# Layer norms: mean and variance from VectorE's statistics instruction on each half, second steps half by half

## The chip, the cores and the metric

One core of one Trainium2 chip runs the whole program; the other seven are idle. The metric is device time in microseconds (us), the median of repeated executions. The engines named below are PE (TensorE, matrix products), DVE (VectorE, elementwise work and reductions along a row), ACT (ScalarE, one-input functions), POOL (GpSimd) and SP (SyncE, which only issues transfers here).

## The reference, cut to what matters

The model is a first block (mixers and a gated feed-forward network with RMS norms) followed by a second block of two layers. All activations are 256 x 1024 in float32. The second block normalizes after each of its three sublayers, so there are six layer norms in all:

```python
def _layer_norm(x, g, b):
    xf = x.astype(F32)
    mu = jnp.mean(xf, axis=-1, keepdims=True)
    xc = xf - mu
    var = jnp.mean(xc * xc, axis=-1, keepdims=True)
    return (xc * lax.rsqrt(var + LN_EPS) * g.astype(F32) + b.astype(F32)).astype(x.dtype)

for i in range(DEPTH_2):          # 2 layers: NSA attention, then HGRN2
    x = _layer_norm(alpha * x + 0.5 * _swiglu(x, ffn1...), ln_gain[i, 0], ln_bias[i, 0])
    y = _nsa(...) if kind == 0 else _hgrn2(...)
    x = _layer_norm(alpha * x + y, ln_gain[i, 1], ln_bias[i, 1])
    x = _layer_norm(alpha * x + 0.5 * _swiglu(x, ffn2...), ln_gain[i, 2], ln_bias[i, 2])
```

## The kernel before, in words

**Tiling.** The 256 positions are two tiles (tt = 0 and 1) of 128 partitions; a row's 1024 features lie along the free axis, in two halves of 512 (hf = 0 and 1), because a product of one tile accumulates in two PSUM banks, `acc[0]` and `acc[1]`.

**Products.** Every weight is split into a high and a low part: ACT copies it to `hi` (line 262), DVE subtracts to get `lo` (line 265), and `bulk_mm` (line 355) multiplies both. `get()` hands out the next weight and splits up to five halves ahead; there are six buffers for `hi` and three for each `lo`, so a split can also wait until PE has used an older weight. The activations are split in the same way: `to_XT` transposes four 128 x 128 blocks on PE (line 513), which is one half of a tile, and `split_to` makes the high part on ACT (line 500) and the low part on DVE (line 503) into `XT`.

**The layer norm.** `ln_tile` is called once for each tile of each of the six norms, so 12 times. It forms `r` = alpha x + product, half by half (line 566, with a running sum into `st`); three steps on one column per row follow (lines 568, 570, 571), which scale the sum to the mean and set the extra column of `r` from which the epsilon comes. ACT then squares the whole centred row of 1025 columns into a scrap tile `jk` and adds it up (line 574); POOL raises the result to the power -1/2 (line 536 in `rsqrt`); DVE subtracts the mean and multiplies by the gain, both halves (line 578, "sub" below), and multiplies by the root and adds the bias, both halves (line 581, "mul" below). `to_XT` transposes the result for the next product; the last norm writes each half to DRAM instead.

**Where the norms stand.** After a feed-forward network (sites A, C, D and, at the end, F) a stock of held products lets PE finish tile 0 long before tile 1. After the two mixers (site B after NSA attention, site E after HGRN2) `Out.last` finishes tile 0 first, and only the remaining products of tile 1 are left for PE (`n1` of 8 steps are already done): `W.last(fin)` calls `finish(tt, ...)`, that is `ln_tile`, after each tile. The next product, `mmB_first`, takes tile 0 for all four weight halves and then tile 1.

**What sets the order.** The instructions are not issued in the order of the text. A planner goes through simulated time and gives each engine, whenever it is free, the ready instruction with the best priority; `tc.high_priority(offset=PRI)` puts the norms ahead of the weight splits around them. The order so planned is then fixed: each engine works through its own queue in that order. `queue_behind(i, other)` adds an edge for order only. `behind(ns, ...)` queues the transposes of `to_XT` behind so many nanoseconds of bulk products; `LNNS` = 4600 for tile 0 and 4300 for tile 1 after a feed-forward network, 0 and 4300 after a mixer, plus 600 for the second half.

Of the kernel before, what the change touches and what calls it, by code (L numbers as in the profile page):

```python
# [9 lines left out]
F32 = mybir.dt.float32  # L10
F32R = mybir.dt.float32r
U32 = mybir.dt.uint32
AF = mybir.ActivationFunctionType
ALU = mybir.AluOpType
# [3 lines left out]
P = 128  # L18
S = 256
D = 1024  # L20
DFF = 2816
NEG = -1e30
ALPHA = 4.0 ** 0.25
# [83 lines left out]
def _kern(ctx, tc, nc, A, out):  # L107
    V, ACT, PE, POOL = nc.vector, nc.scalar, nc.tensor, nc.gpsimd
    cp = ctx.enter_context(tc.tile_pool(name="cp", bufs=1))
    wp = ctx.enter_context(tc.tile_pool(name="wp", bufs=4))  # L110
    xp = ctx.enter_context(tc.tile_pool(name="xp", bufs=2))
# [3 lines left out]
    def nm(s):  # L115
        _n[0] += 1
        return f"{s}_{_n[0]}"


    def new_x(rms=False):  # L120

        t = xp.tile([P, D + 1], F32, tag="x", bufs=3, name=nm("x"))
        if rms:
            POOL.memset(t[:, D : D + 1], 32.0 * 1e-6 ** 0.5)
        return t
# [19 lines left out]
    def queue_behind(i, other):  # L145

        tc.add_manual_dep(i, other.ins.name,
                          mybir.DependencyInfo(mybir.DependencyClass.NoSync, mybir.DependencyReason.DATA))
# [360 lines left out]
    def to_XT(XT, tt, x, k0=0, nk=8, ns=0, gain=None):  # L509
        for q in range(0, nk, 4):  # L510
            w = min(4, nk - q)
            ps = psb()
            ts = [PE.transpose(ps[:, j * P : (j + 1) * P], x[:, (q + j) * P : (q + j + 1) * P], ident) for j in range(w)]  # L513
            if ns:
                behind(ns + 150 * q, [t.ins for t in ts])
            ks = slice(k0 + q, k0 + q + w)
            src = ps[:, : w * P].rearrange("p (a b) -> p a b", a=w)
            if gain is None:
                split_to(XT[:, ks, tt, 0, :], XT[:, ks, tt, 1, :], src)
            else:  # L520
                ACT.activation(XT[:, ks, tt, 0, :], src, AF.Copy, scale=gain)
                V.scalar_tensor_tensor(XT[:, ks, tt, 1, :], src, gain, XT[:, ks, tt, 0, :].bitcast(F32), ALU.mult, ALU.subtract)
# [6 lines left out]
    def rsqrt(src, n, eps):  # L529

        r = xp.tile([P, 16], F32, tag="rsr", bufs=4, name=nm("rsr"))
        if eps:
            v = xp.tile([P, 16], F32, tag="rsv", bufs=4, name=nm("rsv"))
            POOL.tensor_scalar(v[:, :n], src, float(eps), None, ALU.add)
            src = v[:, :n]
        POOL.tensor_tensor(r[:, :n], src, mhalf[:, :n], ALU.pow)  # L536
        return r[:, :n]
# [15 lines left out]
    def load_gb(g, b):  # L553
        t = xp.tile([P, 2, D], F32, tag="gb", bufs=1, name=nm("gb"))
        nc.sync.dma_start(t[:, 0, :], g.partition_broadcast(P))
        if b is not None:
            nc.sync.dma_start(t[:, 1, :], b.partition_broadcast(P))
        return t

    def ln_tile(tt, x, acc, gb, XT, final=False, ns=0):  # L560
        y = new_x()
        r = xp.tile([P, D + 1], F32, tag="r", bufs=2, name=nm("r"))
        st = xp.tile([P, 4], F32, tag="st", bufs=4, name=nm("st"))
        for hf in range(2):
            cs = slice(hf * 512, (hf + 1) * 512)
            V.scalar_tensor_tensor(r[:, cs], x[:, cs], ALPHA, acc[hf], ALU.mult, ALU.add, accum_out=st[:, hf : hf + 1])

        V.tensor_scalar(st[:, 2:3], st[:, 0:1], st[:, 1:2], 1.0 / (32 * D), ALU.add, ALU.mult)

        V.tensor_scalar(r[:, D : D + 1], st[:, 2:3], 32.0, 32.0 * 1e-5 ** 0.5, ALU.mult, ALU.add)  # L570
        V.tensor_scalar(st[:, 3:4], st[:, 2:3], 32.0, None, ALU.mult)
        jk = xp.tile([P, D + 1], mybir.dt.bfloat16, tag="jk", bufs=1, name=nm("jk"))
        var = xp.tile([P, 1], F32, tag="ss", bufs=4, name=nm("var"))
        ACT.activation(jk, r, AF.Square, bias=st[:, 2:3], scale=-1.0 / 32, accum_out=var)  # L574
        rs = rsqrt(var, 1, 0)
        for hf in range(2):
            cs = slice(hf * 512, (hf + 1) * 512)
            V.scalar_tensor_tensor(y[:, cs], r[:, cs], st[:, 3:4], gb[:, 0, cs], ALU.subtract, ALU.mult)
        for hf in range(2):
            cs = slice(hf * 512, (hf + 1) * 512)  # L580
            V.scalar_tensor_tensor(y[:, cs], y[:, cs], rs, gb[:, 1, cs], ALU.mult, ALU.add)
            if final:
                nc.sync.dma_start(out[tt * P : (tt + 1) * P, cs], y[:, cs])
        if not final:
            to_XT(XT, tt, y, ns=ns)
        return y
# [917 lines left out]
    x = list(x0)  # L1504
# [23 lines left out]
    for li in range(2):  # L1528
        gb = load_gb(A["ln_gain_2"][li, 0:1], A["ln_bias_2"][li, 0:1])
        XT, XTn = XTn[0], [newXT()]  # L1530

        def fin(tt, acc, ns):
            with tc.high_priority(offset=PRI):
                x[tt] = ln_tile(tt, x[tt], acc, gb, XTn[0], ns=ns)

        ffn(XT, False, True, fin)
        gb = load_gb(A["ln_gain_2"][li, 1:2], A["ln_bias_2"][li, 1:2])
        XT, MT = XTn[0], newXT()
        W = Out(MT, N1[1 + li])
        (nsa_mix if li == 0 else hgrn_mix)(XT, MT, W)  # L1540
        XTn = [newXT()]
        W.last(fin)
        gb = load_gb(A["ln_gain_2"][li, 2:3], A["ln_bias_2"][li, 2:3])
        XT, XTn = XTn[0], [newXT() if li == 0 else None]
        if li == 1:
            def fin(tt, acc, ns):
                with tc.high_priority(offset=PRI):
                    ln_tile(tt, x[tt], acc, gb, None, final=True)
        ffn(XT, False, True, fin)
# [42 lines left out]
```

## Time and profile before

| | |
|---|---|
| median of 3 executions | 1399.06 us (1398.65 to 1399.69) |
| profiled execution: its own time | 1401.19 us |
| its span, first to last instruction | 1399.0 us |
| PE busy | 1369.6 us (98%) |
| DVE busy | 947.4 us (68%) |
| ACT busy | 721.7 us (52%) |
| POOL busy | 35.6 us (3%) |
| mean granted clock of PE | 0.993 |

The span is what the trace covers; 2.19 us of the profiled execution lie around it. Busy shares are means over stages: an engine with a modest share can be the one that everything waits for in a short stretch.

### The profile page before, as it was taken

How to read it: one execution, taken by the hardware profiler on the slowest of the kernel's cores; microseconds unless marked ns; L12 is line 12 of the kernel's file. 1: busy time of each engine (PE TensorE's matmuls, PEld its weight loads, DVE VectorE, ACT ScalarE, POOL GpSimd, SP SyncE). 2: the span in 40 equal slices, each digit the busy share in tenths (PEclk: the TensorE clock that was granted, in tenths of full speed). 3: DMA queues.
4: the chain of work that ended last, by engine and by line, in shares of the span. 5: the costliest groups of instructions: out<-in, count | busy, mean ns of one | idle time of the engine just before them, and what ended most of it. 6: DMA issues, size and time to landing. Idle time of an engine off the chain costs nothing.

```text
span 1399.0 us, 21630 instructions
## 1 busy us (share of the span) xinstructions
PE 1369.6 (98%) x8649; PEld 1220.1 (87%) x8649; DVE 947.4 (68%) x1611; ACT 721.7 (52%) x1161; POOL 35.6 (3%) x65
## 2 busy tenths in 40 slices
PE   6999999999999999999999999999999999999997
PEld 6988999998888889998888888888889998888886
DVE  4865698877565776786765676555676666755574
ACT  4744544453545643776555463555645443555561
POOL 1010000000000000000000000000000000100000
PEclk9999999999999999999999999999999999999999
DMA  7623866555565665531665573565655332655560
GB/s 223 228 91 111 251 214 208 181 181 170 193 196 193 212 204 148 202 95 56 217 190 197 185 250 136 193 197 187 210 188 181 121 121 92 202 190 181 187 204 30
DMA packets 185427, 245.36 MB, mean 175 GB/s; under 512 B 7408, under 2 KB 164761, under 8 KB 185327
## 3 DMA queue, kind: packets, MB, share of 16 engines
q1 hardware_dynamic: 184511, 240.74, 52.9%
q0 software_dynamic: 816, 3.25, 0.8%
q8 instruction: 68, 1.11, 0.3%
q14 instruction: 32, 0.26, 0.1%
HBM read 242.89 MB, written 4.23 MB: 177 GB/s over the span
## 4 chain that ended last, share of the span: by engine, by line
PE 88%; issue 7%; DVE 2%; POOL 1%; ACT 1%; DMA 1%; SPq 0%; DVEq 0%; POOLq 0%; ACTq 0%
PE psa L355 37%; PE acc L355 23%; PE psb L355 20%; PE psb L513 1%; POOL rsr L536 1%; PE psb L1240 1%; DMA x<-in_x_dram 1%; PE psT L1223 1%; PE psS L1073 1%; PE psb L1242 1%; PE psS L1194 1%; DVE lo L265 0%; ACT hi L262 0%; PE psT L1225 0%; PE lev L1384 0%
## 5 line engine op out<-in xcount | busy, mean ns | idle before, releaser
L265 DVE TENSOR_TENSOR lo<-raw,hi 128x1024 fp32r<-128x1024 f32 x428 | 521.1, 1223 | 268.9 <-ACT hi L262 266.4
L262 ACT ACTIVATE hi<-raw 128x1024 fp32r<-128x1024 f32 x428 | 448.9, 1056 | 379.7 <-PE psa L355 143.1
L355 PE MATMUL psa<-XT,hi 128*128 128x256 f32 (+1 forms) x1632 | 413.5, 328 | 0.0
L355 PE MATMUL psa<-XT,lo 128*128 128x256 f32 x1136 | 321.6, 283 | 0.0
L355 PEld LDWEIGHTS psa<-XT,hi 128*128 128x128 f32 x1632 | 275.0, 188 | 30.2 <-issue 0.6
L355 PE MATMUL psb<-XT,hi 128*128 128x512 f32 (+1 forms) x960 | 283.8, 356 | 0.0
L355 PE MATMUL acc<-hi,H 128*128 128x512 f32 x880 | 280.3, 391 | 0.0
L355 PE MATMUL psb<-XT,lo 128*128 128x256 f32 x800 | 223.6, 279 | 0.0
L355 PEld LDWEIGHTS psa<-XT,lo 128*128 128x128 f32 x1136 | 214.3, 189 | 3.2 <-issue 1.2
L355 PE MATMUL psa<-hi,XT 128*128 128x256 f32 (+1 forms) x928 | 199.4, 304 | 0.6 <-ACT XT L500 0.6
L355 PEld LDWEIGHTS acc<-hi,H 128*128 128x128 f32 x880 | 165.3, 188 | 34.6
L355 PEld LDWEIGHTS psb<-XT,hi 128*128 128x128 f32 x960 | 169.1, 187 | 28.7
L355 PE MATMUL acc<-lo,H 128*128 128x512 f32 x440 | 172.8, 393 | 0.0
L355 PEld LDWEIGHTS psa<-hi,XT 128*128 128x128 f32 x928 | 151.6, 193 | 6.3 <-ACT XT L500 2.0
L355 PEld LDWEIGHTS psb<-XT,lo 128*128 128x128 f32 x800 | 150.2, 188 | 0.0
L355 PE MATMUL psa<-lo,XT 128*128 128x256 f32 (+1 forms) x464 | 130.9, 299 | 0.2 <-DVE lo L265 0.2
L355 PEld LDWEIGHTS acc<-lo,H 128*128 128x128 f32 x440 | 82.8, 188 | 16.7
L355 PEld LDWEIGHTS psa<-lo,XT 128*128 128x128 f32 x464 | 89.8, 194 | 2.4 <-DVE lo L265 0.5
L500 ACT ACTIVATE XT<-psb 128x512 fp32r<-128x512 f32 (+1 forms) x46 | 23.5, 531 | 46.6 <-PE psb L513 46.5
L500 ACT ACTIVATE H<-sg 128x512 fp32r<-128x512 f32 x51 | 31.6, 619 | 29.3 <-DVE sg L625 15.4
L659 ACT ACTIVATE sg<-z 128x512 f32<-128x512 f32 x40 | 25.2, 631 | 40.3 <-DVE z L442 40.1
L574 ACT ACTIVATE jk<-r,st 128x1025 bf16<-128x1025 f32 x12 | 13.9, 1156 | 48.3 <-DVE r L570 24.6
(353 smaller groups left out, 1208.2 us busy)
## 6 DMA issues: line engine op xcount, KB each, us to landing
raw<-in_ffn_w_gate_dram SPq DMA_DIRECT2D x44, 1024.0 KB, 5.1
raw<-in_ffn_w_up_dram SPq DMA_DIRECT2D x44, 1024.0 KB, 5.2
raw<-in_ffn_w_down_dram SPq DMA_DIRECT2D x44, 1024.0 KB, 4.8
raw<-in_w_up_dram SPq DMA_DIRECT2D x22, 1024.0 KB, 4.9
raw<-in_hgrn_w_in_dram SPq DMA_DIRECT2D x16, 1024.0 KB, 5.2
raw<-in_w_down_dram SPq DMA_DIRECT2D x11, 1024.0 KB, 5.2
raw<-in_nsa_w_in_dram SPq DMA_DIRECT2D x10, 1024.0 KB, 5.3
raw<-in_w_in_dram SPq DMA_DIRECT2D x9, 1024.0 KB, 5.0
```

Source lines behind the costliest of these rows:

```text
L262: h = ACT.activation(hi, src, AF.Copy)
L265: i = (POOL if j in pool_halves else V).tensor_tensor(lo, src, hi.bitcast(F32), ALU.subtract)
L355: i = PE.matmul(o, l, r, start=start, stop=stop)
L500: i = ACT.activation(hi, src, AF.Copy)
L513: ts = [PE.transpose(ps[:, j * P : (j + 1) * P], x[:, (q + j) * P : (q + j + 1) * P], ident) for j in range(w)]
L536: POOL.tensor_tensor(r[:, :n], src, mhalf[:, :n], ALU.pow)
L659: ACT.activation(sg, zg, AF.Silu)
L1073: PE.matmul(ph[:, 0:60], w1[:, l % 8, :], d["blk"][kv][:, l].rearrange("p c r n -> p (c r n)"), start=(l == 0), stop=(l == 15))
L1194: PE.matmul(s1, QS[:, j // 2, j % 2, P:S], K[:, u].rearrange("p a b -> p (a b)"), start=(i == 0), stop=(i == 1))
L1223: PE.transpose(pt[:, o : o + P], E1[:, br, sb * P : (sb + 1) * P], ident)
L1240: PE.matmul(po5[:, 1, j % 2, br], T1[:, 2 * br + sb], vv[br][:, sb, vs], start=(sb == 0), stop=(sb == 1))
L1242: PE.matmul(po5[:, 0, j % 2, br], T0[:, br], vv[br][:, 0, vs], start=True, stop=True)
```

## The change

The sum at line 566 is no longer taken. After each half of `r` is formed, DVE's statistics instruction (`bn_stats`) writes six numbers for that half into `st`, and `bn_aggr` joins the two sets to a mean and a variance. A small DVE step adds the epsilon, and POOL takes the power as before. ACT's square is gone, with its scrap tile. The last four DVE steps are put half by half: sub and mul of the first half, then sub and mul of the second, with an edge that keeps sub of the second half behind mul of the first.

```diff
-        st = xp.tile([P, 4], F32, tag="st", bufs=4, name=nm("st"))
+        st = xp.tile([P, 16], F32, tag="st", bufs=4, name=nm("st"))
         for hf in range(2):
             cs = slice(hf * 512, (hf + 1) * 512)
-            V.scalar_tensor_tensor(r[:, cs], x[:, cs], ALPHA, acc[hf], ALU.mult, ALU.add, accum_out=st[:, hf : hf + 1])
-        V.tensor_scalar(st[:, 2:3], st[:, 0:1], st[:, 1:2], 1.0 / (32 * D), ALU.add, ALU.mult)
-        V.tensor_scalar(r[:, D : D + 1], st[:, 2:3], 32.0, 32.0 * 1e-5 ** 0.5, ALU.mult, ALU.add)
-        V.tensor_scalar(st[:, 3:4], st[:, 2:3], 32.0, None, ALU.mult)
-        jk = xp.tile([P, D + 1], mybir.dt.bfloat16, tag="jk", bufs=1, name=nm("jk"))
-        var = xp.tile([P, 1], F32, tag="ss", bufs=4, name=nm("var"))
-        ACT.activation(jk, r, AF.Square, bias=st[:, 2:3], scale=-1.0 / 32, accum_out=var)
-        rs = rsqrt(var, 1, 0)
+            V.scalar_tensor_tensor(r[:, cs], x[:, cs], ALPHA, acc[hf], ALU.mult, ALU.add)
+            V.bn_stats(st[:, 6 * hf : 6 * hf + 6], r[:, cs])
+        V.bn_aggr(st[:, 12:14], st[:, 0:12])
+        V.tensor_scalar(st[:, 14:15], st[:, 13:14], 1e-5, None, ALU.add)
+        rs = rsqrt(st[:, 14:15], 1, 0)
+        done = None
         for hf in range(2):
             cs = slice(hf * 512, (hf + 1) * 512)
-            V.scalar_tensor_tensor(y[:, cs], r[:, cs], st[:, 3:4], gb[:, 0, cs], ALU.subtract, ALU.mult)
-        for hf in range(2):
-            cs = slice(hf * 512, (hf + 1) * 512)
-            V.scalar_tensor_tensor(y[:, cs], y[:, cs], rs, gb[:, 1, cs], ALU.mult, ALU.add)
+            i = V.scalar_tensor_tensor(y[:, cs], r[:, cs], st[:, 12:13], gb[:, 0, cs], ALU.subtract, ALU.mult)
+            if done is not None:
+                queue_behind(i.ins, done)
+            done = V.scalar_tensor_tensor(y[:, cs], y[:, cs], rs, gb[:, 1, cs], ALU.mult, ALU.add)
```

## Rows read from the trace of the kernel before

**Rows 1.** The page, busy time of each engine over the span.

```profile
PE 1369.6 (98%) x8649; PEld 1220.1 (87%) x8649; DVE 947.4 (68%) x1611; ACT 721.7 (52%) x1161; POOL 35.6 (3%) x65
```

**Rows 2.** Stages: us, busy PE, PEld, DVE, ACT, POOL, PE clock, DMA share, GB/s.

```profile
655.00:680.00 25.00, 23.72 (x142) 20.10 (x141) 22.88 (x39) 14.58 (x19) 1.40 (x2) 1.00 0.42 147
841.00:867.00 26.00, 26.00 (x156) 22.98 (x155) 15.52 (x32) 7.60 (x13) 1.10 (x2) 1.00 0.34 121
1190.00:1214.00 24.00, 21.46 (x129) 18.20 (x129) 19.17 (x37) 13.06 (x25) 3.84 (x6) 0.93 0.51 164
```

**Rows 3.** Timeline of PE, tile 0's transposes at sites B and E.

```profile
670.42 1.29 PE L513 MATMUL psb<-ident,x 128*128 128x128 f32 x8 [1.22 <-DVE x L581]
...
1202.80 1.75 PE L513 MATMUL psb<-ident,x 128*128 128x128 f32 x8 [2.00 <-DVE x L581]
```

**Rows 4.** Timeline of all engines at the end of the program, site F.

```profile
1391.03 0.69 DVE L566 SCALAR_TENSOR_TENSOR r<-x,acc 128x512 f32<-128x512 f32 x1 [3.06 <-PE acc L355]
...
1391.76 0.21 DVE L568 TENSOR_SCALAR st<-st 128x1 f32<-128x1 f32 x1
...
1392.26 1.15 ACT L574 ACTIVATE jk<-r,st 128x1025 bf16<-128x1025 f32 x1 [6.97 <-DVE st L571]
1392.26 1.41 DVE L578 SCALAR_TENSOR_TENSOR x<-r,st,gb 128x512 f32<-128x512 f32 x2
...
1393.64 0.54 POOL L536 TENSOR_TENSOR rsr<-var,mhalf 128x1 f32<-128x1 f32 x1 [7.73 <-ACT jk L574]
1394.22 1.41 DVE L581 SCALAR_TENSOR_TENSOR x<-x,rsr,gb 128x512 f32<-128x512 f32 x2 [0.55 <-POOL rsr L536]
```

**Rows 5.** Timeline of DVE at site C, tile 0.

```profile
848.73 0.69 DVE L566 SCALAR_TENSOR_TENSOR r<-x,acc 128x512 f32<-128x512 f32 x1 [2.89 <-PE acc L355]
...
852.49 1.41 DVE L581 SCALAR_TENSOR_TENSOR x<-x,rsr,gb 128x512 f32<-128x512 f32 x2 [0.43 <-POOL rsr L536]
```

**Rows 6.** Chain that ended last, site C: transposes of tile 0's second half.

```profile
855.50 0.44 PE psb L513 x4
```

**Rows 7.** Timeline of DVE at site E, tile 0 and the start of tile 1.

```profile
1197.49 0.68 DVE L566 SCALAR_TENSOR_TENSOR r<-x,psa 128x512 f32<-128x512 f32 x1
...
1198.26 0.69 DVE L566 SCALAR_TENSOR_TENSOR r<-x,psa 128x512 f32<-128x512 f32 x1
...
1199.44 0.69 DVE L566 SCALAR_TENSOR_TENSOR r<-x,acc 128x512 f32<-128x512 f32 x1
...
1200.05 1.41 DVE L578 SCALAR_TENSOR_TENSOR x<-r,st,gb 128x512 f32<-128x512 f32 x2
1201.90 1.42 DVE L581 SCALAR_TENSOR_TENSOR x<-x,rsr,gb 128x512 f32<-128x512 f32 x2 [0.44 <-POOL rsr L536]
```

**Rows 8.** Groups of DVE instructions by form: count, busy us, mean ns, idle before.

```profile
L751 DVE TENSOR_REDUCE ass<-kn 128x8 f32<-128x520 f32 x2 | 1.4, 686 | 0.0
...
L712 DVE TENSOR_SCALAR mT<-mT 128x512 f32<-128x512 f32 x1 | 0.4, 421 | 0.0
...
L1064 DVE TENSOR_TENSOR blk<-psa,posT 64x480 f32<-64x480 f32 x8 | 8.5, 1061 | 4.5 <-PE psa L355 4.4
```

**Rows 9.** Timeline of POOL at site E, tile 0's power.

```profile
1200.76 1.11 POOL L536 TENSOR_TENSOR rsr<-var,mhalf 128x1 f32<-128x1 f32 x1 [6.88 <-ACT jk L574]
```

**Rows 10.** Timeline of DVE at site B, tile 0 and part of tile 1.

```profile
665.84 0.68 DVE L566 SCALAR_TENSOR_TENSOR r<-x,psa 128x512 f32<-128x512 f32 x1
...
669.52 1.41 DVE L581 SCALAR_TENSOR_TENSOR x<-x,rsr,gb 128x512 f32<-128x512 f32 x2 [0.44 <-POOL rsr L536]
...
672.67 0.20 DVE L568 TENSOR_SCALAR st<-st 128x1 f32<-128x1 f32 x1
...
673.51 1.21 DVE L265 TENSOR_TENSOR lo<-raw,hi 128x1024 fp32r<-128x1024 f32 x1
```

**Rows 11.** Stages around the transposes of B and E, columns as in rows 2.

```profile
672.00:674.00 2.00, 2.00 (x18) 1.95 (x18) 2.00 (x8) 0.72 (x2) 0.00 (x0) 1.00 0.00 0
...
1204.00:1205.00 1.00, 1.00 (x6) 0.78 (x5) 0.65 (x2) 0.73 (x2) 0.00 (x0) 0.50 0.00 0
```

## The prediction

> **What bounds the kernel now.** I read the page first: PE is busy 98% of the span [rows 1], so the norms can cost time only where PE stands still for them. The stage table shows where. At site C, as at A and D, PE is busy in all of 26 us, while at B it misses 1.28 us of 25 and at E 2.54 us of 24 [rows 2]. The timeline of PE names the gap: tile 0's transposes come after 1.22 us of waiting at B and 2.00 us at E, both times for mul of line 581 [rows 3]. The fourth place is the end, F: after the last product DVE's work from 1391.03 to 1395.63 is bare, and the store of the last half follows it [rows 4]. So three short stretches decide: B, E and F. At B, moreover, DVE is nearly full, 22.88 of 25 us, while ACT is busy for 14.58 [rows 2]: there the change takes work from the engine with room and gives it to the one without.
>
> At A, C and D the norm has slack. At C, tile 0's second half is ready at 852.49 + 1.41 = 853.90 [rows 5], and its transposes, queued behind bulk products, begin at 855.50 [rows 6].
>
> **Prices.** Two rules come from the timelines. A DVE step that waits for nothing starts 0.08 us before the one in front ends (1199.44 + 0.69 against 1200.05 [rows 7]); so one sub or mul lasts (1.41 + 0.08) / 2 = 0.75 us. A step that waits for the one in front starts 0.04 after its end (1391.72 to 1391.76 [rows 4]).
>
> bn_stats is nowhere in the trace. It reads 512 numbers in each row and writes six. Below lies a one-input step on 128 x 512 at 0.42 us, above the slowest step of that length, 1.06 us for 480 numbers; the reduction of 520 numbers to 8 took 0.69 us [rows 8]. It is the nearest in what it reads and writes, so I take 0.69, with 0.42 and 1.06 for the range. bn_aggr and the step with the epsilon work on a few columns: 0.21 us each, as line 568 [rows 4]; at half or twice that each moves a site by 0.1 to 0.2, inside the bounds of bn_stats.
>
> **What goes.** The three small steps: from 1391.76 to 1392.26, 0.50 us. ACT's square and its readout, with the handoff: from 1392.26 to POOL's start at 1393.64, 1.38 us. But under these ran both subs, 1.41 us [rows 4]. The work that ACT loses is itself worth nothing: at B and E it has idle time, elsewhere PE covers it. The readouts of the running sum (0.08 each) were mostly inside the steps' own time; I count nothing for them.
>
> **What comes.** Per tile DVE gets two bn_stats (0.61 apiece when they don't wait), bn_aggr and epsilon (0.25 + 0.17) and loses 0.50: 1.14 us more. And the edge puts sub of the second half behind mul of the first, which waits for POOL. Before, both subs filled that wait. What is queued behind it now is the whole second half, and the transposes behind that.
>
> The wait is also longer than POOL's 0.54 us [rows 4]. At E the power began at 1200.76, under the second sub (which ended at 1200.05 + 1.41 = 1201.46 [rows 7]), and took 1.11 us [rows 9], to 1201.87: 0.41 after that sub ended. At F nothing ran beside it and it took 0.54. In the new order the power always meets sub of the first half, since DVE goes straight on to it after the epsilon. I therefore let the power end 0.41 after that sub.
>
> The Trainium skill, "SBUF — State Buffer", section "Summary: rules for kernel authors", speaks against the change here: when a VectorE instruction with two SBUF inputs runs beside a GpSimd instruction that reads SBUF, the later to issue is blocked until the first has finished. By that rule the power would run its whole 0.54 us after the sub, 0.13 more per norm than by the row, and the sum below would be about 0.4 us larger, an estimate by that page; the row decides.
>
> **F, worked out.** First step 1391.03 to 1391.72, bn_stats to 1392.45, bn_aggr to 1392.70, epsilon to 1392.95; sub of the first half from 1392.87 to 1393.62, power to 1394.03, mul from 1394.07 to 1394.82; then sub from 1394.74 and mul from 1395.53 to 1396.28. Before: 1395.63. **+0.6 us** (0.65; +0.24 without the meeting on POOL).
>
> **B.** Tile 0 from 665.84 [rows 10] by the same rules, in the order r, r, statistics, statistics: the second bn_stats ends at 668.35, bn_aggr 668.60, epsilon 668.85, sub 669.52, power 669.93, mul 670.72, then sub and mul to 672.18. Before, the mul steps ended at 670.27 and 670.93. The first half comes 0.45 late, the second 1.25; PE's order has all eight transposes ahead of the next product, so 1.25 is lost. Tile 1 has 1.14 more too, partly under tile 0's products: I count 0.5. That is 1.75 if DVE does nothing else meanwhile. But the planner fills the pauses of a chain that waits on itself: on tile 1 at B a weight split of 1.21 us stands between its small steps and its subs (673.51) [rows 10], and at E tile 1's first step stands at 1199.44, ahead of tile 0's subs [rows 7]. The new chain has more pauses: after the second bn_stats, after bn_aggr, before each mul. With a 0.61 us step of tile 1 in each (0.61 + 0.61 + 0.16 + 0.57) tile 0 comes 3.2 late, and tile 1 then costs nothing more. Between 1.75 and 3.2 I take **+2.3 us**: some are filled.
>
> **E.** Here the second half of r starts only at 1198.26, held by PE, so the first bn_stats is nearly free: it pushes that step to 1198.82. Then bn_stats to 1200.24, sub of the first half to 1201.41, power to 1201.82, mul to 1202.61 (before 1202.65), and the second mul to 1204.07 (before 1203.32). The second four transposes began at about 1202.80 + 1.75 / 2 = 1203.68 [rows 3] and would begin 0.15 behind that mul, at 1204.22: +0.54. Unlike before, this has no step of tile 1 in between; with one, as there was, +1.15, with all four +2.5. I take **+1.1 us**.
>
> **A, C, D.** At C the new chain from 848.73 [rows 5] ends at 855.08 instead of 853.90; 0.27 of the slack is left, after 0.15 for the handoff. A step of tile 1 ahead of the last mul would cost 0.57 and so 0.3 of a stall. For the three sites 0 to 0.9; I take **+0.3 us**, one of three. If statistics cost more than 0.82 us this cover is gone everywhere.
>
> **Sum.** 2.3 + 1.1 + 0.3 + 0.6 = 4.3 us. The profiled execution would go from its own 1401.19 us to 1405.5 (span 1399.0 to 1403.3); it lies 2.1 us above the median of the runs, so for the median 1399.06 + 4.3 = **1403.4 us**, 0.3% slower.
>
> **Rivals.**
> *The pauses stay empty.* 1.75 + 0.54 + 0 + 0.65 = 2.9 us at 0.69 per statistics; at 0.42 it falls by 1.0 at B, 0.5 at E and 0.3 at F, to 1.1. So 1400.2 to 1402.0. For it: before, tile 0 at B had none of tile 1's steps in its pauses [rows 10]. Against: its chain was shorter than tile 1's remaining products, the new one is longer. Chance 0.25.
>
> *Cheap statistics, a free POOL, and so a faster kernel.* If bn_stats runs at 0.42 and POOL isn't held by the sub, E's first mul ends at 1201.66, 1.0 earlier. PE's wait shrinks from 2.00 to about 1.0. After 2.00 us its clock fell to 0.50, the level of 1.2 GHz, and 6 products passed in 1 us; after 1.22 us at B the clock stayed at 1.00, 18 in 2 us [rows 3, 11]. Without the fall E gains 0.46 on the transposes and about 0.7 behind them, with an earlier second half some 1.5; B loses 0.3, F nothing: 1397.9 us. It decides below 0.45 us per statistics and only if POOL is free. Against it: the 1.11 us of rows 9. Chance 0.12, of it 0.05 under 1396.3.
>
> *All pauses filled, or dear statistics.* 3.2 + 2.5 + 0.9 + 0.65 = 7.25: 1406.3 us; with B's wait grown to that of E and the same fall of the clock about 1.1 more. At 1.06 us per statistics the sum of 4.3 rises by 1.5 + 0.7 + 0.4 + 1.4 to 8.3: 1407.4 us. Chance 0.13.
>
> *The forecast*, 1401.9 to 1406: chance 0.50. What a measurement can tell here is 0.2%, 2.8 us: 1396.3 to 1401.9 counts as the same. Slower: 0.50 + 0.13 less the lower edge of the forecast, 0.58. Same: 0.37. Faster: 0.05. The range 1399.5 to 1406.5 leaves out most of the cheap case and the upper half of the dear one, some 0.2.
>
> **What would show it.** Right: DVE's busy time up by some 13 us (12 x 1.14), ACT's down by 16; bn_stats near 0.69; powers near 0.9 to 1.1 us at most of the twelve tiles; PE's waits before the transposes grown to about 2.5 at B, a new wait in front of the second four, last mul about 0.6 later after the last product. Wrong: bn_stats at 0.4 or below, powers at 0.54, the first product behind B not later than before, or a gain or loss of PE far from the norms, where the planner may place steps in another order.

## The result and the profile after

The changed kernel takes 1409.48 us (median of 5 executions, 1409.21 to 1411.21). Before, beside it, took 1399.35 (5 executions, 1398.65 to 1402.05). The medians lie 10.1 us apart, where 4.3 were forecast and the range ended at 1406.5; the ratio over all executions is 1.0068, with a 95% interval of 1.0055 to 1.0080. (Ratios below are of this kind, and can differ from those of the medians by some 0.05%; two later executions at a mean granted clock of 0.557 and 0.751, 2245.31 us of before and 1678.51 us of E2, are left out of them.) The profiled execution took 1411.21 us with a span of 1409.4, against 1401.19 and 1399.0 before.

The page after, busy time of each engine, beside [rows 1]:

```profile
PE 1375.4 (98%) x8649; PEld 1222.0 (87%) x8649; DVE 960.9 (68%) x1599; ACT 707.1 (50%) x1137; POOL 39.5 (3%) x65
```

DVE is up by 13.5 us and ACT down by 14.6, about as forecast (13 and 16). PE is busy 5.8 us longer with the same 8649 products: part of the loss lies in slower products and not in waiting, and no term of the sum contains that.

The groups of DVE instructions after, by form (count, busy us, mean ns, idle before):

```profile
L578 DVE SCALAR_TENSOR_TENSOR x<-x,rsr,gb 128x512 f32<-128x512 f32 x24 | 18.0, 748 | 3.7 <-POOL rsr L536 3.5
L575 DVE SCALAR_TENSOR_TENSOR x<-r,st,gb 128x512 f32<-128x512 f32 x24 | 17.9, 745 | 0.0
L568 DVE BATCH_NORM_STATS2 st<-r 128x6 f32<-128x512 f32 x24 | 16.0, 687 | 0.1
...
L569 DVE BATCH_NORM_AGGREGATE st<-st 128x2 f32<-128x12 f32 x12 | 2.5, 207 | 0.2
```

The prices were right: 687 ns for a statistics instruction (taken: 0.69), 207 for the joining one (0.21), 745 and 748 for a sub and a mul (0.75). Line 567 is now r, 568 the statistics, 569 the joining, 570 the epsilon, 575 sub, 578 mul.

The end of the program, timeline of all engines, answers to [rows 4]:

```profile
1400.97 0.69 DVE L567 SCALAR_TENSOR_TENSOR r<-x,acc 128x512 f32<-128x512 f32 x1 [1.47 <-PE acc L355]
...
1402.74 0.74 DVE L575 SCALAR_TENSOR_TENSOR x<-r,st,gb 128x512 f32<-128x512 f32 x1
1402.97 0.92 POOL L536 TENSOR_TENSOR rsr<-st,mhalf 128x1 f32<-128x1 f32 x1 [6.78 <-DVE st L570]
1403.92 0.75 DVE L578 SCALAR_TENSOR_TENSOR x<-x,rsr,gb 128x512 f32<-128x512 f32 x1 [0.43 <-POOL rsr L536]
...
1405.37 0.75 DVE L578 SCALAR_TENSOR_TENSOR x<-x,rsr,gb 128x512 f32<-128x512 f32 x1
```

From r to the end of the last mul it is 1406.12 - 1400.97 = 5.15 us; before it was 4.60. Site F costs 0.55, where 0.65 was worked out. The power took 0.92 us beside sub and ended at 1403.89, that is 0.41 after sub's end at 1403.48: the meeting that the prediction took from [rows 7, 9], at the same price. All twelve powers take 0.92 to 0.99 us. By the Trainium skill, "SBUF — State Buffer", section "Summary: rules for kernel authors", the later of the two would be blocked entirely; by that the power would have ended 0.54 after sub, and the trace differs from it by 0.13.

**Sites B and E.** The timeline of DVE after, tile 0 at B, beside [rows 10]:

```profile
667.99 1.28 DVE L568 BATCH_NORM_STATS2 st<-r 128x6 f32<-128x512 f32 x2
669.19 0.67 DVE L567 SCALAR_TENSOR_TENSOR r<-x,acc 128x512 f32<-128x512 f32 x1
669.77 0.20 DVE L569 BATCH_NORM_AGGREGATE st<-st 128x2 f32<-128x12 f32 x1
670.19 0.69 DVE L567 SCALAR_TENSOR_TENSOR r<-x,acc 128x512 f32<-128x512 f32 x1 [0.21 <-PE acc L355]
670.80 0.15 DVE L570 TENSOR_SCALAR st<-st 128x1 f32<-128x1 f32 x1
670.86 0.74 DVE L575 SCALAR_TENSOR_TENSOR x<-r,st,gb 128x512 f32<-128x512 f32 x1
671.52 0.69 DVE L568 BATCH_NORM_STATS2 st<-r 128x6 f32<-128x512 f32 x1
672.12 0.74 DVE L578 SCALAR_TENSOR_TENSOR x<-x,rsr,gb 128x512 f32<-128x512 f32 x1
672.77 0.75 DVE L575 SCALAR_TENSOR_TENSOR x<-r,st,gb 128x512 f32<-128x512 f32 x1
673.43 0.69 DVE L568 BATCH_NORM_STATS2 st<-r 128x6 f32<-128x512 f32 x1
674.04 0.74 DVE L578 SCALAR_TENSOR_TENSOR x<-x,rsr,gb 128x512 f32<-128x512 f32 x1
```

Every pause of tile 0's chain holds a step of tile 1: both r (669.19 and 670.19, the second even waiting for PE) and both statistics (671.52, 673.43). That was the rival's picture, not the forecast's. From its first r (666.80) to its last mul's end (674.78) tile 0 takes 7.98 us, against 665.84 to 670.93, 5.09, before.

The timeline of PE after, at B and at E, beside [rows 3]:

```profile
673.00 0.63 PE L513 MATMUL psb<-ident,x 128*128 128x128 f32 x4 [2.85 <-DVE x L578]
674.32 0.58 PE L355 MATMUL psa<-hi,XT 128*128 128x256 f32 x1 [0.69 <-ACT XT L500]
...
675.98 1.06 PE L513 MATMUL psb<-ident,x 128*128 128x128 f32 x4
...
1209.53 0.63 PE L513 MATMUL psb<-ident,x 128*128 128x128 f32 x4 [2.85 <-DVE x L578]
1210.84 0.58 PE L355 MATMUL psa<-hi,XT 128*128 128x256 f32 x1 [0.69 <-ACT XT L500]
...
1212.50 1.05 PE L513 MATMUL psb<-ident,x 128*128 128x128 f32 x4
```

The wait before the transposes is 2.85 instead of 1.22 at B and instead of 2.00 at E. The eight transposes are no longer one block: since the halves come apart, the planner puts products of the first half between the two fours, and the first of them waits 0.69 for ACT's copy of the half. And the second four take 1.06 instead of 0.63. The stage windows say why (us, busy PE, PEld, DVE, ACT, POOL, granted clock, DMA share, GB/s), beside [rows 11]:

```profile
672.00:674.00 2.00, 0.63 (x4) 0.42 (x4) 2.00 (x4) 0.33 (x1) 0.00 (x1) 1.00 0.01 4
674.00:676.00 2.00, 1.68 (x8) 1.68 (x9) 2.00 (x5) 0.27 (x1) 0.00 (x0) 0.58 0.00 0
676.00:678.00 2.00, 2.00 (x12) 2.00 (x12) 1.60 (x4) 0.60 (x1) 0.98 (x1) 0.56 0.00 0
678.00:680.00 2.00, 2.00 (x20) 2.00 (x19) 2.00 (x4) 0.00 (x0) 0.00 (x0) 1.00 0.00 0
...
1210.00:1212.00 2.00, 1.31 (x7) 1.16 (x6) 2.00 (x6) 0.60 (x1) 0.00 (x0) 0.56 0.00 0
1212.00:1214.00 2.00, 2.00 (x12) 2.00 (x11) 1.10 (x2) 0.41 (x1) 0.00 (x0) 0.50 0.00 0
1214.00:1216.00 2.00, 2.00 (x11) 2.00 (x11) 1.78 (x4) 0.19 (x1) 0.94 (x1) 0.50 0.00 0
1216.00:1218.00 2.00, 2.00 (x15) 2.00 (x15) 2.00 (x3) 0.00 (x0) 0.05 (x1) 0.74 0.03 7
```

In the column of the clock, 1.00 is the level of 2.4 GHz and 0.50 that of 1.2. At B the clock now falls after the wait, which it did not before; 12 products pass in 2 us instead of 20. What is missing to 1.00, times the window, is (0.42 + 0.44) x 2 = 1.7 us. At E it is (0.44 + 0.50 + 0.50 + 0.26) x 2 = 3.4 us, where the windows of before give (0.24 + 0.50 + 0.11) x 2 = 1.7:

```profile
1202.00:1204.00 2.00, 1.20 (x7) 1.07 (x8) 1.92 (x4) 0.85 (x2) 0.00 (x0) 0.76 0.00 0
1204.00:1206.00 2.00, 2.00 (x10) 1.78 (x9) 1.59 (x6) 0.92 (x2) 0.00 (x0) 0.50 0.00 0
1206.00:1208.00 2.00, 2.00 (x17) 2.00 (x16) 2.00 (x4) 1.25 (x2) 0.61 (x1) 0.89 0.00 0
```

**Where the 10 us lie.** PE runs the same 7,384 products of line 355 in both kernels, so the start of the n-th can be compared: each number below is how far the kernel falls behind the first profile of before over a stretch, in us. (The first 100 us hold the loading at the start, which comes out between 2.1 us earlier and 1.2 later whatever the kernel; a difference of one or two us between two single executions means nothing for that reason.) E1 to E12 are the experiments below.

| kernel | start | networks | A, C, D | B | E |
|---|---|---|---|---|---|
| after | -0.45 | 2.7 | 0.8 | 3.5 | 3.6 |
| E1 after, 32 bytes on | -0.35 | 3.0 | 1.0 | 4.6 | 2.4 |
| E2 before, 32 bytes on | -0.33 | 2.9 | -0.2 | 0.0 | 0.3 |
| E3 no fillers | 0.57 | 2.9 | 0.0 | 3.3 | 2.3 |
| E4 old order of second steps | -1.89 | 2.9 | -0.1 | 3.1 | 1.2 |
| E6 after, old addresses | 0.56 | 0.0 | 1.0 | 3.5 | 2.4 |
| E7 E3 + E4, old addresses | -0.53 | 0.4 | 0.0 | 1.6 | 2.1 |
| E9 before, 64 bytes on | -1.72 | -1.8 | -0.3 | 0.0 | -1.2 |
| E10 old norms at B and E | -1.87 | 0.2 | 1.0 | 0.0 | 0.0 |

("Networks" are the feed-forward networks outside the norms, 101 to 515 us, 690 to 840, 875 to 1042 and 1225 to 1390; where D costs something, its third of A, C and D is taken out of the third stretch.) For after, F's 0.55 comes on top: 3.5 + 3.6 + 0.8 + 2.7 + 0.55 - 0.45 is 10.7 beside 10.4 of the spans.

The networks lose 2.7 us with nothing of the norms in them, the first one ahead of any layer norm. The groups of PE products show which ones, first before, then after:

```profile
L355 PE MATMUL psb<-XT,hi 128*128 128x512 f32 (+1 forms) x960 | 283.8, 356 | 0.0
L355 PE MATMUL acc<-hi,H 128*128 128x512 f32 x880 | 280.3, 391 | 0.0
...
L355 PE MATMUL acc<-lo,H 128*128 128x512 f32 x440 | 172.8, 393 | 0.0
```

```profile
L355 PE MATMUL psb<-XT,hi 128*128 128x512 f32 (+1 forms) x960 | 283.7, 356 | 0.0
L355 PE MATMUL acc<-hi,H 128*128 128x512 f32 x880 | 283.0, 394 | 0.0
...
L355 PE MATMUL acc<-lo,H 128*128 128x512 f32 x440 | 173.9, 395 | 0.0
```

The down products, with H, take 2.7 us more with the high part of the weights and 1.1 more with the low part (the two overlap in time); the products with XT do not change. What the change does to H is to move it: the scrap tile jk is gone and st is larger, so that every tile allocated after them lies 1,952 bytes a partition lower. XT lies ahead of them and stays.

### The profile page after: what moved, and what is told of

The parts are those of the page before. It is cut to its first block, busy times and chain, and to the rows that moved or that the text cites. A ratio compares the mean times of both kernels' runs of the same rounds, so it can differ in the third digit from the quotient of the medians.

```text
span 1409.4 us, 21595 instructions
## 1 busy us (share of the span) xinstructions
PE 1375.4 (98%) x8649; PEld 1222.0 (87%) x8649; DVE 960.9 (68%) x1599; ACT 707.1 (50%) x1137; POOL 39.5 (3%) x65
## 5 line engine op out<-in xcount | busy, mean ns | idle before, releaser
L355 PE MATMUL acc<-hi,H 128*128 128x512 f32 x880 | 283.0, 394 | 0.0
L503 DVE TENSOR_TENSOR H<-sg,H 128x512 fp32r<-128x512 f32 x51 | 35.0, 686 | 5.6 <-ACT H L500 5.6
```

The source lines that it names most:

```text
L355: i = PE.matmul(o, l, r, start=start, stop=stop)
L503: V.tensor_tensor(lo, src, hi.bitcast(F32), ALU.subtract)
```

## The experiments

My theory after this: three things make up the 10 us. At B and E tile 0 comes late, because its chain has gaps that tile 1's steps fill and because the halves are apart; PE's longer stand lets the clock fall; and the move of H slows its products. The rival: the new norms themselves, through DVE's load or POOL, cost time everywhere.

**E1, E2: addresses, first guess.** H began at a multiple of 64 bytes before and lies 32 past one after. E1 is after, E2 before, each with one more 32-byte buffer of a small tile in front of H:

```diff
-        ss = xp.tile([P, 1], F32, tag="ss", bufs=4, name=nm("ss"))
+        ss = xp.tile([P, 1], F32, tag="ss", bufs=5, name=nm("ss"))
```

> The changed kernel with one more 32-byte buffer for the squares' sums, so that every pool behind it, H among them, stands at the address residue (modulo 64 bytes) that it has in the kernel before; the order of instructions is the same on every engine. Theory (a third of the loss is the address of H, on which the down products' weight loads read): a down product steps in 229 ns instead of 232, and the time falls by 2.5 to 4 us to 1405.5 to 1407. Rival (the slower stepping comes from somewhere else): 1409.5 us as without this edit.

> The kernel before with the same one more 32-byte buffer, which moves H from a multiple of 64 bytes to 32 beyond one; no layer norm is touched. Theory (address): down products step in 232 ns, and the kernel gets 2.5 to 4 us slower, 1402 to 1403.5, ratio 1.002 to 1.003. Rival: 1399.4 us, ratio 1.000.

E1 took 1411.68 us, ratio 1.0078 (1.0065 to 1.0090): no faster than after. E2 took 1403.99, 1.0026 (1.0016 to 1.0036), the ratio that was expected, and acc<-hi,H 282.7 us instead of 280.3. So 32 bytes alone slow the kernel before, which the theory of addresses foresaw, but a multiple of 64 does not make after fast (acc<-hi,H 282.8): that form of the theory fell. In E1's profile the clock falls for twice as long at B and half as long at E as in after's, so that the table has 4.6 and 2.4 where after has 3.5 and 3.6, with the same norms.

**E3: no fillers.** E1, with the r steps of tile 1 and the weight splits that are not yet needed queued behind tile 0's last mul:

```diff
+            i = V.scalar_tensor_tensor(r[:, cs], x[:, cs], ALPHA, acc[hf], ALU.mult, ALU.add)
+            if tt:
+                queue_behind(i.ins, tile0[0])
...
+        if j not in pool_halves:
+            lows.append(i)
+            if tile0:
+                queue_behind(i.ins, tile0[0])
```

> The aligned changed kernel, with all steps of tile 1 on DVE, and the weight splits that are not yet due, queued behind the last mul of tile 0, so that nothing stands in the pauses of tile 0's chain. Theory (the pauses were filled with tile 1's steps, which PE does not wait for): at B tile 0's second half comes about 1.8 us earlier, at E as much, PE's wait at B shrinks by 1 us, and the time falls by 2 to 4 us below the aligned kernel, to 1402 to 1405. Rival (DVE's total work sets these stretches, in whatever order): the stall moves to tile 1's transposes and the time stays within 1 us of the aligned kernel.

1408.72 us, 1.0060 (1.0045 to 1.0075), 3.0 under E1. The difference is within the 2 to 4 us of the theory; the time itself is above its 1402 to 1405, since E1 had not become faster. The wait before the transposes fell from 2.85 to 1.56 at B, and yet B cost 3.3. The timeline of PE of E3 shows what stayed:

```profile
672.67 0.63 PE L517 MATMUL psb<-ident,x 128*128 128x128 f32 x4 [1.56 <-DVE x L584]
673.99 0.39 PE L359 MATMUL psa<-hi,XT 128*128 128x256 f32 x1 [0.69 <-ACT XT L504]
...
674.46 1.05 PE L517 MATMUL psb<-ident,x 128*128 128x128 f32 x4
...
677.01 1.22 PE L359 MATMUL psa<-hi,XT 128*128 128x256 f32 x5 [0.43 <-DVE XT L507]
```

The halves still come apart, with the 0.69 between them, the clock still falls (the second four take 1.05), and the copy of tile 0, now behind tile 1's steps on DVE, is 0.43 late.

**E4: old order.** E1 with both subs and then both muls, as before, but the statistics kept:

```diff
-            i = V.scalar_tensor_tensor(y[:, cs], r[:, cs], st[:, 12:13], gb[:, 0, cs], ALU.subtract, ALU.mult)
-            if done is not None:
-                queue_behind(i.ins, done)
-            done = V.scalar_tensor_tensor(y[:, cs], y[:, cs], rs, gb[:, 1, cs], ALU.mult, ALU.add)
+            V.scalar_tensor_tensor(y[:, cs], r[:, cs], st[:, 12:13], gb[:, 0, cs], ALU.subtract, ALU.mult)
+        for hf in range(2):
+            cs = slice(hf * 512, (hf + 1) * 512)
+            V.scalar_tensor_tensor(y[:, cs], y[:, cs], rs, gb[:, 1, cs], ALU.mult, ALU.add)
```

> The aligned changed kernel with the last four steps in the order of before (both subs, then both muls, no edge). Theory (the edge leaves the wait for POOL bare and puts the second half 1.2 us later): the end after the last product shrinks by 0.5 us, tile 0's second half at B and E comes 1.2 us earlier, the time falls by 1.5 to 3 us, to 1403.5 to 1405.5. Rival (half by half lets PE start on the first half sooner, and so pays for itself): the time rises by up to 1 us.

1407.18 us, 1.0054 (1.0040 to 1.0068), 4.5 under E1, more than expected, while the time itself is above the 1405.5 expected. Site F takes 4.50 us from r to the last mul's end, 0.65 less than after and no more than before. A, C and D cost nothing, the 0.69 is gone at B and E; but the wait at B is 2.92 for all eight transposes, and the clock falls behind it (0.71 and 0.50 in the windows from 672 to 676).

**E5, E6: the addresses again.** E5 is before unchanged, profiled once more. E6 is after with the old addresses: the same edit as E1 with bufs=65, which puts the 1,952 bytes back.

> The kernel before, unchanged, profiled once more. If the slow drift of the bulk products belongs to a kernel and its addresses, the 880 products acc<-hi,H of the first group again take 280.3 us of busy time (to within 0.3), as in the first profile of before. If it belongs to the execution, some value between 280 and 283 comes out, as 283.0, 282.8 and 282.7 did in the other kernels.

> The kernel after, with an unused 1,952 bytes a partition put where the scratch tile of the old square stood, so that every tile has the address that it had before. Theory that the drift comes from the addresses: acc<-hi,H falls back from 283.0 to 280.3 us, the sum over the products with H to about 3.5 us less, and the time to 1405.5 to 1407. Theory that the new norms themselves cause the drift: acc<-hi,H stays at 282.7 to 283.0 and the time at 1409 to 1411.

E5: acc<-hi,H 280.9 us, a property of the kernel and not of one execution (0.6 off, a little more than I allowed). E6: 1406.54 us, 1.0042 (1.0028 to 1.0056), acc<-hi,H 280.8, and the networks lose nothing any more, as the theory of addresses gave. So the move is the cause of the drift. It does not depend on the norms, since E2 has it with the old ones: that part of the rival fell.

**E7: old order and no fillers, old addresses.** E3 and E4 together.

> The kernel after with the addresses of before, the old order of the second steps (subtract, subtract, multiply, multiply) and nothing of tile 1 and no weight split before the end of tile 0. My theory that at B the wait, the transposes dealt between products (0.69) and the lower clock (1.7) make up the 3.7, and that the clock falls because the stretch from the last acc product to the steady products is longer or thinner than before: the wait before the eight transposes is 1.6 to 1.9 us at B, no 0.69 behind them, and no fall of the clock at B; B costs 0.4 to 0.8, E 0 to 0.5, F 0, the drift 0 to 3; the time is 1400 to 1404. Rival, that the fall at B comes with any longer wait: B costs 2.2 or more, 1403 to 1407.

1402.85 us, 1.0017 (1.0006 to 1.0029), inside what my theory gave. The timeline of PE at B:

```profile
670.79 1.29 PE L517 MATMUL psb<-ident,x 128*128 128x128 f32 x8 [1.69 <-DVE x L583]
...
674.34 0.85 PE L359 MATMUL psa<-hi,XT 128*128 128x256 f32 x5 [1.04 <-DVE XT L507]
```

```profile
672.00:674.00 2.00, 1.28 (x9) 1.00 (x8) 2.00 (x4) 0.65 (x2) 0.00 (x0) 1.00 0.00 0
674.00:676.00 2.00, 1.66 (x14) 1.66 (x15) 2.00 (x6) 0.00 (x0) 0.91 (x1) 1.00 0.00 0
```

The wait is 1.69, the clock stays at 1.00, and none of the rival's 2.2 or more at B; but B still costs 1.6, twice what I wrote. What I had left out is the 1.04: XT's copy of tile 0 stands on DVE behind r and statistics of tile 1, which were put off until then. At E 2.1 us stay, of which the wait explains nothing (1.92 against 2.00); tile 1's transposes come as one late block there and a product behind them stands 0.90. I took that no further.

A profile shows one execution; the mean granted clock is known of all. What it lacks to 1.00, times the span, is the time lost to the clock, an estimate from three decimals that holds the whole program and not B alone. Its mean is 11.5 us in after, 12.7 in E1 and 11.0 in E4 and in E6, whose profiles wait 2.85 to 2.92 us at B; it is 8.4 in E3 (1.56) and in E7 (1.69), and 8.2 to 9.0 in the sets of before. So the kernels with the long wait lose 2 to 4 us more to the clock than before. For E3 none is seen, though with five executions its mean is uncertain by more than 1 us: two of them, and four of the twelve of E7, reach 0.996, the clock of E9 and E12, in whose profiles it falls neither at B nor at E. E3's fall at B is thus shown for the profiled execution and not for all.

**E8, E9, E11, E12: before at other addresses.** The edit of E2 with bufs=6 (64 bytes: E8 one execution, E9 twelve), 8 (128 bytes, E11, one execution) and 10 (192 bytes, E12, one execution).

> The kernel before with its later tiles 64 bytes higher (two more buffers of one small tile). Theory that an address of 0 modulo 64 makes the products with H fast: acc<-hi,H stays at 280.3 us. Rival, that a finer pattern of the address or of the execution sets it: 282 to 283 us, as with 32 bytes.

> The kernel before with its later tiles 64 bytes higher, timed. If what one look showed (1395.87) belongs to the kernel, it is faster than before by 1 to 4 us: acc<-hi,H at 279.7 where before has 280.3 to 280.9 gives 1 to 2, and E without a fall of the clock 1.7 more. If it was that execution's luck, it is within 1 us of before.

> The kernel before with its later tiles 128 bytes higher: H lies at 64 modulo 256, as in the aligned after, where acc<-hi,H took 282.8. If the address modulo 256 sets it, 282.5 to 283; if not, 279.5 to 281.

> The kernel before with its later tiles 192 bytes higher: H lies at 128 modulo 256. No value measured there: 279.5 to 281 if every address of 0 modulo 64 but 64 is fast, 282 to 283 otherwise.

E9: 1398.77 us beside 1399.76, ratio 0.9988 (0.9978 to 0.9999): 1.0 us by the medians and 1.7 by the ratio, at the border between a faster kernel and that execution's luck. The single executions took 1395.87 (E8), 1405.26 (E11) and 1399.52 us (E12). E12 is no slower than before although its networks lose 2.0 us, because its start comes 2.1 earlier and its clock does not fall at E. Over all kernels, by H's start modulo 256 (from the compiled program):

| H modulo 256 | acc<-hi,H, us for 880 products | kernels |
|---|---|---|
| 0 | 279.7, 279.4 | E8, E9 |
| 192 | 280.3, 280.9, 280.8, 280.5, 280.6 | before, E5, E6, E7, E10 |
| 128 | 282.4 | E12 |
| 224 | 282.7 | E2 |
| 64 | 282.8, 282.9, 282.8, 282.8 | E1, E3, E4, E11 |
| 32 | 283.0 | after |

Two positions are fast and four are slow; at 192 and at 64, where both norms were measured, the norm makes no difference. E9 to E12 ran on one chip and show both paces, so the chip is not the cause. E12 refutes that every multiple of 64 but 64 is fast. The gate tiles and the held weights move along with H, so which of them PE feels is not separated.

**E10: old norms at B and E alone.** After with the old `ln_tile` for the third, fourth, ninth and tenth call, and H 256 bytes above its place in before:

```diff
+        calls.append(tt)
+        if (len(calls) + 1) // 2 in (2, 5):
+            return ln_old(tt, x, acc, gb, XT, final, ns)
```

> The kernel after with the old norms at B and E alone (four of the twelve tiles), and its later tiles 256 bytes above where before has them. Theory that B and E carry the loss and the addresses the drift: what stays is F (0.55) and some 0.3 each at A, C and D, so 1.0 to 1.8 us over before. Rival, that the new norms cost something all over: 4 us or more over before.

1400.41 us beside 1399.76, ratio 1.0001 (0.9992 to 1.0009): 0.7 us by the medians and 0.1 by the ratio, under the 1.0 to 1.8 expected, of which the interval holds the lower part. With B and E as before and the addresses at a fast place, the loss is gone within that interval. In the profile A, C and D cost 0.3 each, as expected.

## Why the prediction came out as it did

The direction was right, and the size was not: 10.1 us instead of 4.3. Two steps failed. The sum put the products far from the norms at nothing, and they lost 2.7 us by the move of H. And it counted PE's standing time alone, at full clock, while the clock fell at B, where it had not before, and for twice as long at E, 1.7 us each in after's profile. By site the loss there is 3.5 at B (2.3 forecast), 3.6 at E (1.1), 0.8 at A, C and D (0.3), 0.55 at F (0.6) and 2.7 in the networks (0).

- **Prices, F, the meeting on POOL:** right, to 0.1 us at F, where the epsilon took 0.15 and not 0.21. In all DVE stood 3.5 us before the mul steps for the power, less than the 4.8 before, because at B and E steps of tile 1 now fill that wait.
- **B, the wait:** 2.3 forecast; 2.85 - 1.22 = 1.6 and the 0.69 for ACT's copy make 2.3. That the sum agrees is luck, since its working is not right. "Some are filled" was wrong, all four pauses are; and "PE's order has all eight transposes ahead of the next product" did not hold in the new order, since the planner moved seven products up as soon as the halves came apart.
- **B, the clock:** a step that failed. The sum held only PE's standing time, at full clock. The fall of the clock was in a rival, at 1.1 us and a chance of 0.13; it came, with 1.7. With the waits this makes 4.0 where 3.5 were lost: the 0.69 is not all loss, since four transposes that stood ahead of the first product now come behind it. With 2.85 to 2.92 us of wait the clock falls at B in every profile (after, E1, E4, E6), in either order of the second steps; with 1.56 and two blocks 0.69 apart it falls in E3's profile, with 1.69 and one block it stays in E7's. By the mean clocks above, the kernels with the long wait are those that lose more to the clock; that the split blocks matter to it is not shown.
- **E:** 1.1 forecast. 2.85 - 2.00 = 0.85 and 0.69 are 1.5 of waits; the other 1.7 of after's profile is a second half-clock stretch of the same length. E6, with the same norms, has only the one that before has too, (0.47 + 0.38) x 2 = 1.7, and E costs 2.4. So the second is not certain in every execution. The waits leave 0.4 of after's 3.6 and 0.9 of E6's 2.4 over. In both a product waits 0.30 us for ACT's copy of tile 1, which none does in before, and the forecast had no term for tile 1 at E; the rest stays open.
- **A, C, D:** 0.3 forecast, 0.8 to 1.0 measured, 0.3 at each: the step of tile 1 ahead of the last mul, which the prediction gave one site of the three, comes at all of them. With the old order (E4) or no fillers (E3) it is gone.
- **The networks:** the other step that failed, 2.7 us that no term held, and what carries the time out of the range. The prediction named a loss of PE far from the norms as a sign against it, but expected it from the planner's order. It came from the freed scratch tile. In time, E6 against after is 0.26% of the kernel less (two comparisons whose intervals touch), 3.6 us, in which the shorter fall at E has its part; E2 shows the address by itself at 0.26% too.

The experiments thus split the loss: without the address term the change costs 1.0042, 5.8 us, which would lie inside the forecast's range (1399.06 + 5.8 = 1404.9). Of that, in the profiles, half-by-half order and fillers are each enough to keep most of the loss at B (3.1 to 3.5 us with either, 1.6 with neither); but E3's 3.3, the order without fillers, holds a fall of 1.7 that not all its executions have, so for the order alone this is not shown. By the times, with 0.26% taken off for the address, E3 keeps 0.34% and E4 0.28%, between the 0.42% of E6 and the 0.17% of E7, and the intervals do not tell the two apart. What stays open is why E loses 2.1 in E7, and what decides at the margin whether the clock falls.

## What to carry to other kernels

When an engine waits a little longer at a place where its clock is near a fall, price the fall as well as the wait: here 1.7 us beside 2.3 of waits, in the profile of after at B. Splitting a chain into halves opens gaps, and a planner fills them with other work that then stands in front of the critical step; look at what it would put there before counting an earlier first half as a gain. A change that frees or resizes a buffer moves every later one: put the addresses back, as E6 does, before judging the change by its time.

## What the hardware showed that I had not expected

The pace of TensorE's products depends on where in SBUF the tiles lie that moved with H: 279.4 to 283.0 us for the same 880 products, by H's start address modulo 256 as in the table. 64 bytes more bring these products in the kernel before from 280.3 to 279.4 us; the whole kernel gained 0.12%, in which executions without a fall of the clock at E may have their part.

The same wait does not always bring the clock down. In E9 the transposes at E wait 2.00 us, as in before, and come in the same block of eight:

```profile
1199.31 1.29 PE L513 MATMUL psb<-ident,x 128*128 128x128 f32 x8 [2.00 <-DVE x L581]
```

```profile
1200.00:1202.00 2.00, 1.97 (x15) 1.74 (x16) 1.83 (x7) 1.17 (x2) 0.00 (x0) 1.00 0.00 0
1202.00:1204.00 2.00, 2.00 (x19) 2.00 (x18) 2.00 (x6) 1.25 (x2) 0.51 (x1) 1.00 0.00 0
1204.00:1206.00 2.00, 2.00 (x20) 2.00 (x19) 2.00 (x4) 0.00 (x0) 0.34 (x1) 1.00 0.00 0
```

The clock stays at 1.00 here, and 19 or 20 products pass in 2 us where before had 10 from 1204 to 1206. Of the eight profiles with the old norm at E, all with a wait of 1.99 or 2.00 us and eight transposes behind it, the clock falls there in five (before, E2, E5, E10, E11) and stays in three (E8, E9, E12). The executions of before in that comparison scatter with their mean clock, from 1398.21 us at 0.995 to 1403.64 at 0.991; where in the program it fell in them is not recorded.
